# Feed-forward products as seven half-size block products, with x streamed from DRAM

## The chip, the cores and the metric

One Trainium2 chip, one program on all 8 cores (two dies, cores 0 to 3 and 4 to 7). The time is device microseconds of the slowest core. Most executions agree within a few tenths of a per cent; in some, cores of one die run at a lower granted TensorE clock and the time is longer. Those are called slow runs here and are not compared with fast ones.

## The reference

Two layers of a diffusion backbone; in each, four token mixers run side by side and a squared-ReLU MLP follows. Each core takes its own 1280 tokens (1024 context, 256 latent) through all the weights.

```python
D_MODEL = 2048; D_FF = 4 * D_MODEL
def _layer(x, cond, lw, h0, lat):
    mod = (jax.nn.silu(cond) @ w_mod + b_mod)[:, None, :]      # 6 D values: "modulation"
    sh1, sc1, g1, sh2, sc2, g2 = jnp.split(mod, 6, axis=-1)
    h = _rms(x) * (1 + sc1) + sh1
    proj = h @ w_in
    ...   # four mixers, their gates, and the merge
    x = x + g1 * (merged @ w_out)
    h2 = _rms(x) * (1 + sc2) + sh2
    x = x + g2 * (jnp.square(jax.nn.relu(h2 @ w_ff1)) @ w_ff2)  # the feed-forward
    return x, k, v, s_fin
```

## The kernel before

The program writes operations with priorities; a list scheduler of its own orders them on every engine and places semaphores. Activations lie as feature blocks (partitions) by 1280 tokens, in f16; x in f32 (80 KB a partition) stays in SBUF during the feed-forward. A weight block of 128 rows comes through a ring of buffers, cast from f32 by the GpSimd queue.

```python
NRING = 7
def dense(srcs, act, evac, group=1, ...):       # per block: 16 matmuls each of 512, 512, 256 columns
    ...
    for tgi, (t0, n) in enumerate(TGS):
        dense_tile(ws[0], W16, act, t0, n, evac, g[0][0], tgi, ...)
    if hook is not None: hook()                 # hk = mod_step: a modulation round after each block

# feed-forward of a layer: four quarters of D_FF, up (w1) then down (w2)
for q in range(4):
    dense(b1, hT, ev_f1, tag="ff1", hook=hk)                    # 16 blocks: relu^2 into mT
    dense(b2, mT, ev_res(l, 80, None), tag="ff2", hook=hk)      # 16 blocks: x = psum*g2 + x
    ...   # first stage in groups of five blocks; last stage with norm and output

def mod_kc(l, s, kc, st):                       # a modulation round: 1 MB of w_mod, 4 small matmuls
    w = ring(wm[l, s, kc], tag="wmod")
    ...
    if kc == 15:
        tm = A(180 + 8, [16, 32], F32)          # its transpose: a tile shared with other scratch
...
# start: load x, sums of squares, 32 modulation rounds, then normalise
mod_step(32)
for tgi in range(3): norm_tile(0, 0, tgi)
...
S.pools["ps"].allow = {..., "d": (4, 5, 6, 7), "s": (0, 1, 2), "g": (4, 6), "mod": (3,), "G": (4, 6, 0, 2)}
```

Of the kernel before, what the change touches and what calls it, by code (L numbers as in the profile page):

```python
# [40 lines left out]
class Pool:  # L41
    def __init__(self, n, view, psum=False):
        self.n = n
        self.view = view
        self.psum = psum
        self.free = [0.0] * n
        self.busy = [False] * n
        self.last = [None] * n
        self.live = {}
        self.quota = {}  # L50
        self.allow = {}
        self.seq = None
        self.ptr = 0

    def take(self, vt):
        if self.seq is not None and self.seq[self.ptr] is not vt:
            return False
        c = vt.cls
        if c in self.quota and self.live.get(c, 0) + vt.nb > self.quota[c]:
            return False  # L60
        best = None
        for s in self.allow.get(c) or range(0, self.n - vt.nb + 1, vt.nb):
            if any(self.busy[s + i] for i in range(vt.nb)):
                continue
            k = max(self.free[s + i] for i in range(vt.nb))
            if best is None or k < best[0]:
                best = (k, s)
        if best is None:
            return False
        s = best[1]  # L70
        self.ptr += 1
        vt.slot = s
        vt.prev = []
        for i in range(vt.nb):
            self.busy[s + i] = True
            if self.last[s + i] is not None:
                vt.prev.append(self.last[s + i])
            self.last[s + i] = vt
        self.live[c] = self.live.get(c, 0) + vt.nb
        return True  # L80
# [12 lines left out]
class Graph:  # L93
# [123 lines left out]
    def schedule(self):  # L217
        ops = self.ops
        for o in list(ops):
            for v in o.new:  # L220
                if self.pools[v.pool].psum:
                    mine = set(v.ops)
                    for i in v.ops:
                        if ops[i].eng != "pe":
                            o.preds.update(p for p in ops[i].preds if p not in mine and p < o.id)
        for pool in self.pools.values():
            if not pool.psum:
# [249 lines left out]
NRING = 7  # L477
TOTKB = 207.5
# [37 lines left out]
def build():  # L516
# [39 lines left out]
    with es:  # L556
# [52 lines left out]
        acc1 = cal([768], F32)  # L609
# [5 lines left out]
        keep = cal([2, 10])  # L615
        lsm = cal([202])
# [5 lines left out]
        mhalf = cal([16])  # L622
        dtv = cal([10, 16])
        dtA = cal([10, 16])
        E = cal([6, 10, 8])
        wgt = cal([2, 10, 8])
        ssn = cal([2, 10])
        stt = [cal([10]) for _ in range(6)]
        ssv = [cal([2]) for _ in range(8)]
        assert cb[0] <= TOTKB  # L630

        xT = A(40, [16, T], F32)
# [4 lines left out]
        tmpi = [0]  # L637

        def tmp16(dt=F16):
            tmpi[0] = (tmpi[0] + 1) % 4  # L640
            v = TMP[tmpi[0]]
            return v if dt == F16 else v.bitcast(dt)
# [9 lines left out]
        def load(dst, src, nb, q="sp", r=(), w=None, prio=None, tag="ld"):  # L652
            S.dma(q, dst, src, nb, r=r, w=[dst] if w is None else w, prio=(S.p if prio is None else prio) - 60.0, tag=tag)
# [27 lines left out]
        def dense(srcs, act, evac, group=1, tag="mm", hook=None, cls="D"):  # L681

            i = 0
            while i < len(srcs):
# [8 lines left out]
                else:  # L693
# [3 lines left out]
                    for (b, s), w in zip(g, ws):  # L697
                        for tgi in (1, 2):
                            dense_tile(w, W16, act, TGS[tgi][0], TGS[tgi][1], evac, b, tgi, tag=tag, cls=cls)
                        S.p += UNIT * 0.6  # L700
# [84 lines left out]
        def mod_kc(l, s, kc, st):  # L785
# [3 lines left out]
            w = ring(wm[l, s, kc], tag="wmod")  # L789

            def f(e):
                ins = None
                for j in range(4):
                    ins = e.matmul(ps.ap()[32 * j:32 * j + 32, :], lhsT=scT[:, kc, :], rhs=w.ap(F16)[:, 512 * j:512 * j + 512], start=kc == 0, stop=kc == 15)  # L794
                return ins
            S.op("pe", 0.24, f, r=[w, scT], w=[ps], tag="mod")
            if kc == 15:
                tm = A(180 + 8, [16, 32], F32)
# [20 lines left out]


        acc0 = A(38, [512], F32)

        def accv(a, b):
            return acc0[:, a:b] if b <= 512 else acc1[:, a - 512:b - 512]

        def sq_acc(fc, t0, n, first):
            t = tmp16(BF16)[:, 0:n]
            xv = xT[:, fc, t0:t0 + n]
            av = accv(t0, t0 + n)
            if first:  # L830
                act_op(av, xv, AF.Square, n, [xv], [av])
            else:
                act_op(t, xv, AF.Square, n, [xv], [t])
                tt("dve", av, av, t, ALU.add, n, [av, t], [av])

        def norm_rstd(c0, c1, k):

            nck = c1 - c0
            ps = PS("n")

            def f(e):
                ins = None
                for c in range(c0, c1):
                    ins = e.matmul(ps.ap()[:, c - c0:c - c0 + 1], lhsT=accv(c * 128, c * 128 + 128), rhs=ones_f[:, 0:1], start=True, stop=True)  # L844
                return ins
            S.op("pe", 0.3 * nck, f, r=[accv(c0 * 128, c1 * 128), ones_f], w=[ps], tag="norm")
# [3 lines left out]
            S.op("pool", 0.6, lambda e: e.tensor_tensor(out=rv, in0=sv, in1=mhalf[:, 0:nck], op=ALU.pow), r=[sv, mhalf], w=[rv])  # L850
            ps2 = PS("n")
            for c in range(c0, c1):
                dg = tmp16(F32)[:, 0:128]
# [4 lines left out]
        def norm_apply(l, which, t0, n, ps2):  # L858
            jsh, jsc = (0, 16) if which == 0 else (48, 64)
            s = 0 if t0 < 1024 else 1  # L860
            for fc in range(16):
                t = tmp16()[:, 0:n]
# [7 lines left out]
        def norm_tile(l, which, tgi):  # L870
            t0, n = TGS[tgi]
            ps2 = norm_rstd(t0 // 128, (t0 + n) // 128, tgi)
            norm_apply(l, which, t0, n, ps2)
# [154 lines left out]
        def fourier(l):  # L1028
            alt = [0]

# [3 lines left out]
            dense([(g, wf[l, g]) for g in range(4)], hT, ev, tag="fproj", cls="d")  # L1034
# [62 lines left out]
        def gmlp(l):  # L1097
# [4 lines left out]
            def vt(t):  # L1102
# [3 lines left out]
                S.p += 3.5  # L1106
                vg = gelu2(ps, 512, None, "gelv")
# [9 lines left out]
            for b in range(4):  # L1117
                dense([(b, wu[l, b])], hT, ev_u, tag="uproj", cls="d")
# [20 lines left out]
        def ssm_proj(l):  # L1139
# [22 lines left out]
            dense([(b, wx[l, b]) for b in (4, 5, 6, 7, 0, 1, 2, 3)], hT, ev, tag="xproj", cls="d")  # L1162
# [10 lines left out]
            for t in range(NT):  # L1173
# [3 lines left out]
                S.p += 3.5  # L1177
                zv = ztok[:, t, :]
# [297 lines left out]
        def reload_x(fcs, l):  # L1476
            for fc in fcs:
                load(xT[:, fc, :], (xin if l == 0 else xs)[fc], 128 * T * 4, r=[] if l == 0 else ["xs%d" % fc], tag="xld")

        def layer(l):  # L1480
            last = l == NL - 1
            S.tag = "mix"
            layer_consts(l)
            attn_proj(l)
# [9 lines left out]
            hk = mod_step  # L1494
# [4 lines left out]
            reload_x(order, l)  # L1499
# [3 lines left out]
            def after_o(blk, tgi, t0, n):  # L1503
                sq_acc(blk, t0, n, tgi not in seen)
                seen.add(tgi)
                if blk == order[-1] and tgi in (0, 2):
                    if tgi == 0:
                        norm_tile(l, 1, 0)
                    else:
                        norm_tile(l, 1, 1)  # L1510
                        norm_tile(l, 1, 2)
            ev = ev_res(l, 32, after_o)
            dense([(b, wo[l, b]) for b in order[:11]], mT, ev, tag="wout", hook=hk)
            dense([(b, wo[l, b]) for b in order[11:]], mT, ev, group=5, tag="wout", hook=hk)
            while modq and modq[0][0] == l:
                mod_step()
            if not last:
                mod_push(l + 1, range(6))
            seen2 = set()

            def ev_f1(blk, tgi, t0, n, ps):
                r = tmp16()[:, 0:n]
                act_op(r, lambda: ps.ap()[:, 0:n], AF.Relu, n, [ps], [r], boost=BOOST)
                a = mT[:, blk, t0:t0 + n]
                stt_(a, r, 1.0 / 16, r, ALU.mult, ALU.mult, n, [r], [a], boost=BOOST)

            def after_f(blk, tgi, t0, n):
                if last:
                    S.dma("sp", y_o[blk][:, t0:t0 + n], xT[:, blk, t0:t0 + n], 128 * n * 4, r=[xT[:, blk, t0:t0 + n]])
                    return  # L1530
                sq_acc(blk, t0, n, tgi not in seen2)
                seen2.add(tgi)
                S.dma("sp", xs[blk][:, t0:t0 + n], xT[:, blk, t0:t0 + n], 128 * n * 4, r=[xT[:, blk, t0:t0 + n]], w=["xs%d" % blk] if tgi == 0 else ["xs%d" % blk])
                if blk == 15 and tgi in (0, 2):
                    if tgi == 0:
                        norm_tile(l + 1, 0, 0)
                    else:
                        norm_tile(l + 1, 0, 1)
                        norm_tile(l + 1, 0, 2)
            for q in range(4):  # L1540
                b1 = [(b, w1[l, q * 16 + b]) for b in range(16)]
                if q == 0:
                    dense(b1[:5], hT, ev_f1, group=5, tag="ff1", hook=hk)
                    dense(b1[5:], hT, ev_f1, tag="ff1", hook=hk)
                else:
                    dense(b1, hT, ev_f1, tag="ff1", hook=hk)
                b2 = [(b, w2[l, q, b]) for b in range(16)]
                if q < 3:
                    dense(b2, mT, ev_res(l, 80, None), tag="ff2", hook=hk)
                else:  # L1550
                    while modq:
                        mod_step()
                    e2 = ev_res(l, 80, after_f)
                    dense(b2[:11], mT, e2, tag="ff2")
                    dense(b2[11:], mT, e2, group=1 if last else 5, tag="ff2")

        setup()
        for fc in range(16):
# [3 lines left out]
        for fc in range(16):  # L1562
            for tgi, (t0, n) in enumerate(TGS):
                sq_acc(fc, t0, n, fc == 0)
        mod_step(32)
        for tgi in range(3):
            norm_tile(0, 0, tgi)
        mod_push(0, (2, 3, 4, 5))
        for l in range(NL):
            layer(l)  # L1570
        S.pools["ps"].allow = {"as": (0,), "av": (2, 3), "d": (4, 5, 6, 7), "s": (0, 1, 2), "g": (4, 6), "mod": (3,), "G": (4, 6, 0, 2)}
# [222 lines left out]
```

## Time and profile before

| | kernel before |
|---|---|
| time | 5205 us median of three runs |
| TensorE busy | 95% of the span |
| feed-forward, layer 0 / layer 1 | 1178 / 1165 us, counted from the norm in front of it; TensorE without a gap once the hole after that norm is over |
| mixers, layer 0 / layer 1 | 555 / 551 us |
| gates, merge and output projection, layer 0 / layer 1 | 746 / 717 us (at full clock) |
| start to first attention projection | 215 us |

The feed-forward is 45% of the span and, but for these holes, purely TensorE. The lines that carry this are in the prediction. One more, on the start: a table of 20 us windows (columns: window, length, then busy us and instructions of PE, PEld, DVE, ACT, POOL; granted clock, DMA share, GB/s).

```profile
60.00:80.00 20.00, 7.40 (x48) 4.65 (x48) 7.44 (x19) 4.87 (x11) 5.36 (x9) 1.00 0.56 111
80.00:100.00 20.00, 3.73 (x28) 0.90 (x28) 0.00 (x0) 0.00 (x0) 3.17 (x6) 1.00 1.04 166
100.00:120.00 20.00, 4.29 (x28) 0.92 (x28) 0.98 (x3) 0.00 (x0) 3.51 (x7) 1.00 1.03 172
```

DMA is saturated from 80 us on with modulation weights. There is a short dip from 60 to 80 us, where x has come and the norm runs.

### The profile page before, as it was taken

What the parts mean: (1) busy time and instruction counts of PE and PEld (TensorE: products, weight loads), DVE (VectorE), ACT (ScalarE), POOL (GpSimd) and SP (SyncE); (2) the same over time, 40 slices, a digit from 0 to 9 for tenths busy, and PEclk for the clock granted to TensorE, in tenths of its full rate; (3) what the DMA queues carried; (4) which work ended last, traced back from release to release, by engine and by line L of the source; (5) the groups of instructions that cost most, each with busy time, mean ns of one, the idle gap of its engine ahead of it and who ended that gap; (6) DMA issues with size and microseconds to landing.
All of it is one profiled execution on the core that took longest, in us unless ns stands there. A gap on an engine that the chain in (4) does not pass through costs nothing.

```text
span 5229.1 us, 71536 instructions; the slowest of 8 cores (5194.4 to 5229.1 us)
## 1 busy us (share of the span) xinstructions
PE 4942.5 (95%) x27836; PEld 2557.1 (49%) x27836; DVE 1803.3 (34%) x3060; ACT 1128.2 (22%) x2062; POOL 684.1 (13%) x1044
## 2 busy tenths in 40 slices
PE   1699989999998999999998998999999899999999
PEld 0334444455554555555554344455555455555555
DVE  2446681122242222222245467522223422222222
ACT  1356341111122010010123654311111310101010
POOL 1220241111101111111004013300000000000000
PEclk9999998899998999999999999999999899999999
DMA  9431356665645666666353321544334233333334
GB/s 198 96 69 28 59 124 127 122 132 109 117 79 91 115 117 117 114 119 111 65 137 71 59 46 32 126 91 100 61 63 94 47 62 61 61 61 61 61 66 112
DMA packets 168954, 468.01 MB, mean 90 GB/s; under 512 B 18736, under 2 KB 54064, under 8 KB 168368
## 3 DMA queue, kind: packets, MB, share of 16 engines
q0 software_dynamic: 106560, 368.10, 40.3%
q1 hardware_dynamic: 62064, 95.34, 5.6%
q8 instruction: 228, 3.74, 0.3%
q14 instruction: 102, 0.84, 0.1%
HBM read 792.09 MB, written 39.32 MB: 159 GB/s over the span
## 4 chain that ended last, share of the span: by engine, by line
PE 87%; DVE 3%; issue 3%; DMA 3%; POOL 2%; ACT 1%; SPq 1%; DVEq 0%; POOLq 0%; ACTq 0%
PE psum L664 81%; DVE arena L724 2%; DMA arena<-wm 1%; PE psum L1059 1%; PE psum L794 1%; PE psum L999 1%; PE psum L1017 1%; POOL arena L947 1%; ACT arena L714 1%; PE psum L1019 1%; SPq L215 1%; DVE arena L728 1%; DMA arena<-lc 1%; DMA arena<-wf 0%; POOL arena L724 0%
## 5 line engine op out<-in xcount | busy, mean ns | idle before, releaser
L664 PE MATMUL psum<-arena 128*128 128x512 f16 (+1 forms) x24320 | 4533.1, 347 | 37.6 <-ACT arena L714 15.1
L664 PEld LDWEIGHTS psum<-arena 128*128 128x128 f16 x24320 | 2367.1, 98 | 2105.8 <-issue 231.1
L714 ACT ACTIVATE arena<-psum 128x512 f16<-128x512 f32 (+4 forms) x970 | 515.9, 532 | 3132.9 <-PE psum L664 3043.2
L728 DVE SCALAR_TENSOR_TENSOR arena<-arena 128x512 f16<-128x512 f16 (+8 forms) x569 | 369.9, 656 | 957.3 <-ACT arena L714 924.7
L728 DVE SCALAR_TENSOR_TENSOR arena<-arena,psum 128x512 f16<-128x512 f16 (+4 forms) x492 | 297.9, 606 | 1040.7 <-ACT arena L714 1039.9
L728 DVE SCALAR_TENSOR_TENSOR arena<-psum,arena 128x512 f32<-128x512 f32 (+1 forms) x480 | 316.7, 661 | 890.5 <-PE psum L664 889.2
L724 DVE TENSOR_TENSOR arena<-arena 128x512 f32<-128x512 f32 (+7 forms) x796 | 454.4, 589 | 192.2 <-ACT arena L714 126.5
L714 ACT ACTIVATE arena<-arena 128x512 f16<-128x512 f16 (+8 forms) x489 | 297.6, 652 | 515.4 <-DVE arena L728 317.4
L215 POOL DMA_DIRECT2D arena<-w x256 | 136.0, 531 | 1319.7 <-PE psum L664 1269.1
L215 POOL DMA_DIRECT2D arena<-wm x192 | 103.2, 540 | 1173.7 <-PE psum L794 1020.5
L714 ACT ACTIVATE arena<-psum,arena 128x512 bf16<-128x512 f32 x320 | 202.3, 684 | 128.0 <-PE psum L999 127.8
L724 POOL TENSOR_TENSOR arena<-arena 128x512 bf16<-128x512 bf16 (+2 forms) x160 | 183.9, 1167 | 194.8 <-DVE arena L724 97.7
L215 POOL DMA_DIRECT2D arena<-wg x128 | 72.6, 569 | 862.0 <-PE psum L664 570.1
L794 PE MATMUL psum<-arena 128*32 128x512 f16 x768 | 84.0, 434 | 75.0 <-DMA arena<-wm 74.4
L724 DVE TENSOR_TENSOR arena<-arena,psum 128x512 f16<-128x512 f32 (+2 forms) x232 | 130.6, 607 | 24.0 <-PE psum L855 20.4
L738 ACT COPY arena<-psum 128x512 f16<-128x512 f16 (+5 forms) x148 | 70.1, 491 | 117.1 <-PE psum L664 36.7
L724 DVE TENSOR_TENSOR arena<-psum,arena 128x512 f32<-128x512 f32 (+3 forms) x166 | 80.7, 503 | 41.9 <-POOL arena L947 36.0
L794 PEld LDWEIGHTS psum<-arena 128*32 128x32 f16 x768 | 20.9, 95 | 134.8 <-issue 134.7
L739 DVE CAST arena<-psum 128x512 f16<-128x512 f32 (+4 forms) x102 | 52.6, 523 | 93.5 <-PE psum L1059 73.0
L844 PE MATMUL psum<-arena 128*128 128x1 f32 x80 | 12.5, 274 | 71.0 <-DVE arena L724 68.0
L1024 DVE RECIPROCAL arena<-psum 128x256 f32<-128x256 f32 x40 | 70.2, 1755 | 10.5 <-PE psum L1019 9.7
L1017 PE MATMUL psum<-arena 128*64 128x512 bf16 (+1 forms) x352 | 68.2, 387 | 0.0
(87 smaller groups left out, 918.9 us busy)
## 6 DMA issues: line engine op xcount, KB each, us to landing
arena<-w POOLq DMA_DIRECT2D x256, 512.0 KB, 5.3
arena<-wm POOLq DMA_DIRECT2D x192, 512.0 KB, 6.2
arena<-wg POOLq DMA_DIRECT2D x128, 512.0 KB, 6.8
arena<-xin SPq DMA_DIRECT2D x32, 640.0 KB, 20.4
arena<-wb POOLq DMA_DIRECT2D x64, 256.0 KB, 7.2
arena<-wo POOLq DMA_DIRECT2D x32, 512.0 KB, 5.3
arena<-xs SPq DMA_DIRECT2D x16, 640.0 KB, 7.1
arena<-dftA SPq DMA_DIRECT2D x16, 512.0 KB, 11.9
```

The costliest lines, as they stand in the source:

```text
L215: return self.op(q, issue, (lambda e, o=out, a=in_, k=kw: e.dma_start(out=lz(o), in_=lz(a), **k)), r, w, prio, dma=nbytes, q=q, tag=tag)
L664: ins = e.matmul(o, lhsT=lhs(kc), rhs=rhs(kc), start=kc == 0, stop=kc == nk - 1)
L714: return e.activation(out=lz(o), in_=lz(i), func=func, scale=scale, **kw)
L724: lambda e: e.tensor_tensor(out=lz(o), in0=lz(a), in1=lz(b), op=op), r=r, w=w, prio=S.p - boost, tag=tag)
L728: lambda e: e.scalar_tensor_tensor(out=lz(o), in0=lz(a), scalar=sc, in1=lz(b), op0=op0, op1=op1),
L738: return S.op("act", tact(n), lambda e: e.copy(out=lz(o), in_=lz(i)), r=r, w=w, prio=S.p - boost, tag=tag)
L739: return S.op(eng, tpool(n) if eng == "pool" else tdve(n, ps, x), lambda e: e.tensor_copy(out=lz(o), in_=lz(i)), r=r, w=w, prio=S.p - boos ...
L794: ins = e.matmul(ps.ap()[32 * j:32 * j + 32, :], lhsT=scT[:, kc, :], rhs=w.ap(F16)[:, 512 * j:512 * j + 512], start=kc == 0, stop=kc == 15)
L947: S.op("pool", 0.6, lambda e, rs=rs, ss=ss: e.tensor_tensor(out=rs, in0=ss, in1=mhalf[:, 0:10], op=ALU.pow), r=[ss, mhalf], w=[rs], prio=S ...
L999: ins = e.matmul(sc.ap()[:, hf * 512:hf * 512 + n], lhsT=kT[64 * hf:64 * hf + 64, kb * 128:(kb + 1) * 128], rhs=qT[64 * hf:64 * hf + 64, j ...
L1017: ins = e.matmul(pv.ap()[64 * hf:64 * hf + 64, 0:n], lhsT=V[:, kb, 64 * hf:64 * hf + 64], rhs=PT[:, hf, 0:n], start=ki == 0, stop=ki == nk ...
L1024: S.op("dve", 0.0066 * 256 + 0.1, lambda e, sm=sm, b=b: e.reciprocal(out=rec, in_=sm.ap()[:, 256 * b:256 * b + 256]), r=[sm], w=[rec], tag ...
```

## The change

Intent: take columns off TensorE. Two row blocks of weights (halves A11, A12 and A21, A22) times two halves of the tokens and of the contraction need eight block products. The Winograd form of Strassen's algorithm needs seven, with four sums of weights, four of activations and seven sums of results. A unit of two blocks so becomes 112 matmuls of 320 columns.

The sums of activations take the place of x in SBUF. So x goes to DRAM after the output projection, and the down stages load, update and store it in parts of 128 x 320 elements. To make room and keep engines free, modulation rounds leave the feed-forward, the weight ring shrinks from 7 to 6, scratch tiles and PSUM banks are dealt out anew, and the start is reordered.

```diff
-NRING = 7
+NRING = 6
+        TMX = cal([16, 32])
+        HTs = [A(40 + 10 * i, [8, 640]) for i in range(4)]     # sums of activations, in x's place
+        ATs = [A(80 + 10 * i, [8, 640]) for i in range(4)]
+        SL = [A(184 + 2 * i, [1024]) for i in range(4)]        # sums of weights
+        def sunits(units, act, Ts, epi, pre=None, tag="st"):
+            ...   # next unit's two weight blocks and sums a unit ahead
+                prods = (("X", w8(ra, 0), ra, "B11", True), ("Y", k8(s2), s2, 1, True), ("V", k8(s3), s3, 2, True), ("Z", k8(s1), s1, 0, True),
+                         ("X", w8(ra, 1), ra, "B21", False), ("Z", k8(s4), s4, "B22", False), ("V", w8(rb, 1), rb, 3, False))
+            ...   # each for two token parts of 320; VectorE adds the results
+            XSt = [hT[:, i, 640:1280].bitcast(F32) for i in range(8)]      # buffers for x: one unit
+            def pre_f2(ba, bb):
+                ...   load(XSt[s_ * 4 + k], xs[blk][:, c:c + SUBS], ...)
+            def epi_f2(dst):
+                ...   x = XSt[s_ * 4 + k];  res(x, b, ps, *gcol(blk), c);  spill(blk, c, SUBS, x, dst)
             for q in range(4):
-                    dense(b1, hT, ev_f1, tag="ff1", hook=hk)
-                    dense(b2, mT, ev_res(l, 80, None), tag="ff2", hook=hk)
+                    sunits([pair1(i) for i in range(8)], hT, HTs, epi_f1, tag="sf1")
+                    sunits([pair2(i) for i in range(8)], mT, ATs, epi_f2(...), pre=pre_f2, tag="sf2")
...   modulation: out of the feed-forward
-            hk = mod_step
+            hk = mod_hook                                       # does nothing
+        mod_spread(96, 11.0)                                    # before layer 0's mixers
+                mod_spread(64, 15.0)                            # in layer 1's mixers
-                tm = A(180 + 8, [16, 32], F32)
+                tm = TMX
...   norm: the diagonal for the broadcast is in the same tile
-                dg = tmp16(F32)[:, 0:128]
+                dg = TMX.rearrange("p a b -> p (a b)")[:, 128 * (c - c0):128 * (c - c0) + 128]
...   mixers: Fourier projection first, in a group of four
-        S.pools["ps"].allow = {..., "d": (4, 5, 6, 7), "s": (0, 1, 2), "g": (4, 6), "mod": (3,), "G": (4, 6, 0, 2)}
+        S.pools["ps"].allow = {..., "d": (4, 5, 6), "s": (0, 1, 6), "g": (2, 4), "mod": (7,), "G": (0, 2, 4)}
```

## The prediction

> **What bounds the kernel now.** I read first the page's busy shares and its chain of work that ended last, then a table of busy time by stage, then the matmuls of one long stage by shape, and last the DMA queues.
>
> ```profile
> PE 4942.5 (95%) x27836; PEld 2557.1 (49%) x27836; DVE 1803.3 (34%) x3060; ACT 1128.2 (22%) x2062; POOL 684.1 (13%) x1044
> PE 87%; DVE 3%; issue 3%; DMA 3%; POOL 2%; ACT 1%; SPq 1%; DVEq 0%; POOLq 0%; ACTq 0%
> PE psum L664 81%; DVE arena L724 2%; DMA arena<-wm 1%; PE psum L1059 1%; PE psum L794 1%; PE psum L999 1%; PE psum L1017 1%; POOL arena L947 1%; ACT arena L714 1%; PE psum L1019 1%; SPq L215 1%; DVE arena L728 1%; DMA arena<-lc 1%; DMA arena<-wf 0%; POOL arena L724 0%
> ```
>
> TensorE carries 87% of the chain, the dense matmuls of one helper (L664) 81% of the span. By stage (columns: window, length, busy us and instructions of PE, PEld, DVE, ACT, POOL, granted clock, DMA share, GB/s):
>
> ```profile
> 0.00:160.00 160.00, 24.26 (x152) 9.80 (x152) 33.36 (x85) 26.58 (x53) 22.59 (x44) 1.00 0.96 196
> 195.00:780.00 585.00, 539.79 (x3178) 250.98 (x3177) 364.41 (x558) 266.98 (x489) 169.34 (x199) 0.96 0.34 69
> 780.00:1040.00 260.00, 260.00 (x1330) 128.02 (x1328) 49.76 (x98) 32.74 (x62) 26.91 (x51) 0.89 0.64 127
> 1560.00:1600.00 40.00, 21.32 (x112) 11.31 (x111) 24.73 (x55) 22.98 (x39) 6.07 (x10) 0.66 0.66 114
> 1600.00:2750.00 1150.00, 1149.69 (x6534) 606.07 (x6533) 285.81 (x478) 137.99 (x255) 116.53 (x219) 1.00 0.59 110
> 4068.00:4117.00 49.00, 26.91 (x161) 17.63 (x160) 37.23 (x75) 34.80 (x57) 4.43 (x7) 0.76 0.33 54
> 4117.00:5229.00 1112.00, 1109.36 (x6143) 601.32 (x6141) 242.87 (x384) 101.55 (x194) 63.94 (x121) 1.00 0.37 67
> ```
>
> The feed-forward stages (1600 to 2750, 4117 to 5229) have no idle TensorE time, full clock, VectorE at 22 to 25% and DMA at 37 to 59%. What takes columns away from TensorE there shortens the kernel one for one, until something else fills. Idle TensorE lies elsewhere: in the DMA-bound start (24 busy of 160 us), in the mixers, and in two holes of some 20 us (1560, 4068) between output projection and feed-forward.
>
> The chain in order of time gives the last stage as one piece, 6144 matmuls (128 weight blocks of 32 of 512 columns and 16 of 256) in 1109.97 us: 8.67 us a block, 180.7 ns a matmul.
>
> **What the Trainium skill says.** "TensorE: Matmul & The Clock Gate", section "Wait — 56ns, not 53.3ns?": warm matmuls start every N / 2.4 GHz + 2.5 ns. So 215.8 ns at 512 and 109.2 at 256; two to one that is 180.3, and the trace has 180.7. For 320 columns I take 135.8 ns, an estimate from that section. Part 1 of the page warns that dense matmuls on three cores of a die bring the clock to 13/16 for as long as they last. Here it came in part, 0.89 from 780 to 1040, and in no feed-forward stage with all eight cores dense; I budget full clock there. "VectorE: DVE Perf Modes", section "Mode 2×_1P": 16-bit operands in SBUF give two results a cycle, PSUM and fp32 one. The trace agrees: 441 ns for an f16 sum of 512, 753 in f32. "HBM Reference", section "Specifications": some 358 GB/s for each core when both of a pair stream. From 70 to 150 us the trace had 164 GB/s written as f16, so 328 read, at full DMA share.
>
> **The change part by part.**
>
> 1. Columns. One unit (two row blocks, both token halves) was 2 x 16 x 1280 = 40960 columns in 96 matmuls: 17.31 us. It becomes 7 products x 2 parts x 8 matmuls of 320: 112 x 135.8 ns = 15.21 us. Saved: 2.10 us. Layer 0 has 29 units up and 28 down (6 and 8 blocks stay dense), layer 1 29 and 32: 118 units, **-247 us**, all on the path.
>
> 2. What the products cost elsewhere, in 15.2 us. Durations at 320, 640 and 1024 elements are interpolated from the groups by shape: PSUM multiply-add 750 and 482 ns at 512 and 256, so 549; PSUM sum 681 and 416, so 482; f16 sum 441 and 300, so 511 at 640 and 722 at 1024. VectorE: 10 PSUM sums 4.8 us, 4 weight sums 2.9, and either 4 activation sums 2.0 (up: 9.7 us, 64%) or 8 residuals 4.4 plus 0.4 for the cut at token 1024 (down: 12.5 us, 82%). ScalarE, up: 16 operations of about 0.46 and 2 copies, 8.3 us. All below 15.2, beside TensorE.
>
> 3. x from DRAM. A down unit loads and stores 8 parts of 164 KB: 2.62 MB, beside two weights of 0.52 MB (as written). The queues of before:
>
> ```profile
> q0 software_dynamic: 106560, 368.10, 40.3%
> q1 hardware_dynamic: 62064, 95.34, 5.6%
> ```
>
> The casting queue moved 368.1 MB in 40.3% of 5229 us, 175 GB/s when busy; the plain one 326 GB/s. A down unit so takes 6.0 + 8.0 = 14.0 us of DMA in 15.2 (92%), an up unit 40%. HBM: 2.1 + 2.6 MB in 15.2 us, 310 GB/s a core, under the 358. It fits, barely. A reload needs its buffer's store to land (2 to 3 us here), yet is used a whole unit later; weights are fetched a unit ahead; up stages work off a backlog.
>
> 4. PSUM. A unit holds all 8 banks, but the banks which a product takes were last read at least two products (4.3 us) before, and a bank read in between and added to again has one product of slack. Evacuations are 0.5 to 1.1 us. I allow **+10 us** at the eight passages from up to down, where the last activation sums are needed about 2 us after their inputs, and **+20 us** for DMA and VectorE bursts in 56 streamed units, some 0.35 us each.
>
> 5. The two holes. At 1567 TensorE waits until 1592: the first up matmuls stand behind norm work, because both use the same four scratch tiles. The change gives them their own tiles and norms each token group by itself; five blocks of the first group (80 x 215.9 ns = 17.3 us) now lie over the rest. I take 20 of some 25 us each: **-40 us**.
>
> 6. The start. It stays DMA-bound: 0.96 share to 160 us, same bytes, so the modulation ends near 145 instead of 153. x is scaled by the norm during the wait, and the rest goes to two engines. The attention projections began at 211; I put them at about 185: **-25 us**.
>
> 7. Modulation of later steps: 160 rounds of 4 small matmuls. Each costs 0.42 us among dense work (9.09 us from block to block in layer 0, 8.67 in layer 1). The order of instructions has 96 of them inside layer 0's feed-forward before and none after; about 60 go into the mixers, whose gaps hide a part: **-15 us**.
>
> 8. The mixers lose one of four PSUM banks for projections (given to modulation) and the gate merge one of four bank pairs; the ring of weights shrinks from 7 to 6. **+10 us**.
>
> Sum: 5205 - 247 + 30 - 40 - 25 - 15 + 10 = 4918; I say **4915 us**, 5.6% less.
>
> **The rivals.**
>
> - The down stages become bound by DMA or VectorE. For: 92% and 82% worked out; VectorE is in order, so a late x holds the PSUM sums behind it. Against: a unit of prefetch, and up stages at 40%. If 56 units took 17 us, as dense, the time would be about 5010.
> - The clock: busier neighbours bring the 13/16 state into the product stages. For: it appears here from 780 to 1040. Against: the gate merge from 1040 had random dense data at 0.58 DMA share and clock 1.00. At 0.89 over 1795 us of products it costs 220 us: about 5130.
> - The chain of additions behind each product stalls TensorE by half a microsecond a unit: +60 us, about 4975. Against: the slack of part 4.
> - The other way: holes and modulation vanish wholly, no stall: about 4865.
>
> **Range and chances.** The columns are arithmetic; the side gains have an uncertainty of some 30 us, stalls another 40, mostly upward. So 4855 to 4990. Faster than 5101 fails only under the clock rival or two rivals at once: faster 0.96, within 2% 0.03, slower 0.01.
>
> **What would show it.** Right: 13216 matmuls of 320 columns at 135 to 137 ns each, units of 15.2 to 15.6 us with TensorE fully busy; DMA near 0.9 in down stages, 0.4 in up stages, VectorE near 80 and 65%; no wait over 5 us at either hole; attention projections by 190 us. Wrong: TensorE waits on VectorE or on x inside down stages, their units above 16 us; clock under 0.97 in product stages; mixers longer than 585 and 630 us.

## The result and the profile after

The changed kernel took 5009 us (median of four runs, the slow one of 5124 us among them; fast runs 4995.94, 5005.90, 5012.84). Before, in the same rounds: fast runs 5204.38, 5205.36 and 5234.69 us. The ratio is 0.960, 95% interval 0.956 to 0.965. A ratio here is the mean time of one kernel's fast runs over that of the other's of the same rounds, so not quite the ratio of the medians. A second job gave 0.962 (0.956 to 0.968). So the kernel is 4% faster, where the prediction had 5.6%, and 5009 us, like every single run, lies above its range of 4855 to 4990 us.

The page of the changed kernel:

```profile
PE 4663.9 (93%) x29724; PEld 2736.0 (55%) x29724; DVE 2584.2 (52%) x4975; ACT 1465.2 (29%) x2951; POOL 696.3 (14%) x1044
...
q0 software_dynamic: 106560, 368.10, 44.4%
q1 hardware_dynamic: 200304, 263.18, 16.9%
...
PE 74%; DMA 12%; DVE 5%; issue 4%; POOL 2%; SPq 1%; ACT 1%; another core or an unknown queue 0%; DVEq 0%; POOLq 0%; ACTq 0%
PE psum L684 42%; PE psum L1623 25%; DMA xs<-arena 6%; DVE arena L744 3%; DMA arena<-xs 3%; DMA arena<-wm 2%; PE psum L1114 1%; SPq L222 1%; DVE arena L748 1%; PE psum L1053 1%; DMA arena<-xin 1%; PE psum L820 1%; PE psum L1071 1%; ACT arena L734 1%; POOL arena L1001 1%
...
L1623 PE MATMUL psum<-arena 128*128 128x320 f16 x13216 | 1807.3, 299 | 35.8 <-DVE arena L744 25.3
...
arena<-xs SPq DMA_DIRECT2D x448, 160.0 KB, 5.4
...
xs<-arena SPq DMA_DIRECT2D x384, 160.0 KB, 6.5
```

L1623 are the new products, L684 the dense helper. The 13216 matmuls are there (118 units of 112). TensorE fell from 87 to 74% of the chain, and DMA rose from 3 to 12%: stores of x (6%) and loads of x (3%) are on the path, which were not there at all. The last two lines give the median time from issue to landing: 5.4 us for the loads and 6.5 us for the stores.

Windows of the changed kernel (columns as before; core 1, the slowest), in order: mixers of layer 0, the two places where the holes were, and two down stages.

```profile
226.00:796.00 570.00, 517.68 (x3124) 237.48 (x3122) 356.28 (x545) 261.60 (x476) 182.36 (x219) 0.97 0.45 85
...
1560.00:1600.00 40.00, 40.00 (x225) 22.55 (x224) 27.05 (x59) 30.35 (x55) 4.54 (x7) 1.00 0.46 99
...
3968.00:4010.00 42.00, 42.00 (x235) 23.54 (x234) 28.71 (x64) 31.98 (x59) 4.50 (x7) 1.00 0.47 98
...
4110.00:4225.00 115.00, 114.16 (x840) 81.75 (x839) 79.63 (x171) 12.97 (x30) 8.06 (x15) 1.00 0.85 198
...
4355.00:4465.00 110.00, 104.90 (x768) 74.32 (x767) 69.66 (x149) 12.13 (x28) 7.53 (x14) 1.00 0.78 181
```

The holes are gone (40 busy of 40 us, 42 of 42). The down stages have full clock, DMA at 0.78 to 0.85 and VectorE at 63 to 69%, both below what the prediction had, and still TensorE loses time there.

Where the time went, by stage. The mean over the cores of the duration between two landmarks among the matmuls: the first of 272 columns (attention projections), the last of 128 columns before the gates, the first of the norm's sums of squares (for the gates of layer 0 before, die 1 alone, since die 0 ran at a clock of about 0.9 there), in us:

| stage | before | after | difference | predicted |
|---|---|---|---|---|
| start to attention projections | 214.8 | 224.4 | +10 | -25 |
| mixers, layer 0 | 555.3 | 569.7 | +14 | |
| gates to output projection, layer 0 | 745.8 | 751.0 | +5 | |
| feed-forward, layer 0 | 1178.0 | 1025.1 | -153 | |
| norm to attention, layer 1 | 72.5 | 77.2 | +5 | |
| mixers, layer 1 | 551.5 | 571.0 | +20 | |
| gates to output projection, layer 1 | 717.5 | 733.6 | +16 | |
| feed-forward, layer 1 | 1165.2 | 1031.5 | -134 | |
| both feed-forwards | | | -287 | -297 (247 columns, 40 holes, 40 modulation, less 30 stalls) |
| mixers, gates and the norm between | | | +60 | +35 (25 modulation, 10 banks and ring) |
| sum | | | -217 | -287 |

The feed-forward did nearly what was predicted. 70 us went elsewhere: 35 in the start, 25 in mixers and gates, 10 in the feed-forward. The rest of the distance is the choice of the slowest core: the fast runs before had it 5 us above this table's mean of 5201, the profiled run after 11 us above 4984, since the cores now stall at different times.

The start. Windows of the changed kernel, and then its TensorE instructions in order of time (start, length, instruction, in brackets what it waited for):

```profile
80.00:100.00 20.00, 3.81 (x17) 3.79 (x18) 6.64 (x20) 5.27 (x13) 1.04 (x1) 1.00 0.53 144
100.00:120.00 20.00, 13.26 (x84) 7.55 (x83) 14.28 (x31) 0.00 (x0) 5.65 (x10) 1.00 0.09 14
...
160.00:180.00 20.00, 3.08 (x20) 0.69 (x20) 2.99 (x8) 2.02 (x3) 3.10 (x6) 0.50 1.04 184
```

```profile
94.58 1.83 PE L896 MATMUL psum<-arena 128*128 128x1 f32 x8 [94.58 <-DVE arena L744]
...
99.72 0.78 PE L907 MATMUL psum<-arena 128*128 128x128 f32 x2
...
114.01 0.76 PE L907 MATMUL psum<-arena 128*128 128x128 f32 x2 [0.54 <-DVE arena L753]
114.70 1.90 PE L820 MATMUL psum<-arena 128*32 128x512 f16 x16
```

From 100 to 120 us DMA is at 0.09: idle, in the one stage that is bound by DMA. The first modulation matmuls (L820) start only at 114.7 us, behind all matmuls of the norm (L896 and L907), which themselves wait for x until 94.6 us. All 15 buffers for modulation weights are full by then, and none comes free before L820 has read it.

The down stages. First the waits of SyncE's queue, which issues loads and stores of x, then those of VectorE, both from 4110 to 4225 us (engine, line, waited for: us in total, times, longest):

```profile
SPq L436 <- DVE arena L748: 84.2, 5, 81.5
SPq L438 <- DMA xs<-arena: 38.4, 21, 4.6
```

```profile
DVE arena L748 <- DMA arena<-xs: 18.2, 12, 3.8
DVE arena L744 <- PE psum L1623: 12.1, 15, 2.2
```

The queue waits 38 us of 115 for stores to land before it may load into the same buffer (the 81.5 us of the first line began before this window, in the up stage). VectorE in turn waits 18 us for x. An example from VectorE's instructions in order of time, 4396 to 4401 us:

```profile
4396.11 0.48 DVE L744 TENSOR_TENSOR arena<-psum,arena 128x320 f32<-128x320 f32 x1
4400.47 0.55 DVE L748 SCALAR_TENSOR_TENSOR arena<-arena 128x320 f32<-128x320 f32 x1 [3.88 <-DMA arena<-xs]
```

For 3.88 us a late x holds up VectorE, and with it the sums behind it for which TensorE needs its banks. In the whole program TensorE waits 25 us for those sums (the page's line of L1623).

### The profile page after: what moved, and what is told of

Its sections match the earlier page's. It is cut to its first block, busy times and chain, and to the rows that moved or that the text cites. A ratio compares the mean times of both kernels' runs of the same rounds, so it can differ in the third digit from the quotient of the medians.

```text
span 4994.4 us, 84152 instructions; the slowest of 8 cores (4969.1 to 4994.4 us)
## 1 busy us (share of the span) xinstructions
PE 4663.9 (93%) x29724; PEld 2736.0 (55%) x29724; DVE 2584.2 (52%) x4975; ACT 1465.2 (29%) x2951; POOL 696.3 (14%) x1044
## 3 DMA queue, kind: packets, MB, share of 16 engines
q0 software_dynamic: 106560, 368.10, 44.4%
q1 hardware_dynamic: 200304, 263.18, 16.9%
## 4 chain that ended last, share of the span: by engine, by line
PE 74%; DMA 12%; DVE 5%; issue 4%; POOL 2%; SPq 1%; ACT 1%; another core or an unknown queue 0%; DVEq 0%; POOLq 0%; ACTq 0%
PE psum L684 42%; PE psum L1623 25%; DMA xs<-arena 6%; DVE arena L744 3%; DMA arena<-xs 3%; DMA arena<-wm 2%; PE psum L1114 1%; SPq L222 1%; DVE arena L748 1%; PE psum L1053 1%; DMA arena<-xin 1%; PE psum L820 1%; PE psum L1071 1%; ACT arena L734 1%; POOL arena L1001 1%
## 5 line engine op out<-in xcount | busy, mean ns | idle before, releaser
L684 PE MATMUL psum<-arena 128*128 128x512 f16 (+2 forms) x12992 | 2452.2, 347 | 23.9 <-ACT arena L734 10.7
L684 PEld LDWEIGHTS psum<-arena 128*128 128x128 f16 x12992 | 1252.4, 98 | 1115.3 <-issue 109.9
L1623 PE MATMUL psum<-arena 128*128 128x320 f16 x13216 | 1807.3, 299 | 35.8 <-DVE arena L744 25.3
L1623 PEld LDWEIGHTS psum<-arena 128*128 128x128 f16 x13216 | 1290.6, 98 | 552.0 <-issue 51.5
L744 DVE TENSOR_TENSOR arena<-arena 128x1024 f16<-128x1024 f16 (+9 forms) x1648 | 923.6, 579 | 237.1 <-ACT arena L734 144.3
L734 ACT ACTIVATE arena<-arena 128x320 f32<-128x320 f32 (+8 forms) x1374 | 680.9, 518 | 893.6 <-DVE arena L744 458.8
L744 DVE TENSOR_TENSOR arena<-psum,arena 128x320 f32<-128x320 f32 (+4 forms) x1346 | 656.6, 490 | 426.8 <-PE psum L1623 304.7
L748 DVE SCALAR_TENSOR_TENSOR arena<-arena,psum 128x512 f16<-128x512 f16 (+3 forms) x492 | 298.3, 607 | 1044.4 <-ACT arena L734 1044.0
L734 ACT ACTIVATE arena<-psum 128x512 f16<-128x512 f32 (+6 forms) x738 | 382.9, 520 | 1390.0 <-PE psum L684 1305.4
L758 ACT COPY arena<-psum 128x320 f32<-128x320 f32 (+6 forms) x384 | 170.0, 448 | 1026.8 <-DVE arena L748 547.1
L748 DVE SCALAR_TENSOR_TENSOR arena<-arena 128x320 f32<-128x320 f32 (+10 forms) x665 | 354.7, 554 | 217.8 <-DMA arena<-xs 131.3
L820 PE MATMUL psum<-arena 128*32 128x512 f16 x768 | 80.0, 424 | 62.5 <-DMA arena<-wm 49.4
L896 PE MATMUL psum<-arena 128*128 128x1 f32 x80 | 11.9, 267 | 96.2 <-DVE arena L744 94.6
L820 PEld LDWEIGHTS psum<-arena 128*32 128x32 f16 x768 | 21.1, 97 | 129.6 <-issue 128.4
```

The costliest lines, as they stand in the source:

```text
L684: ins = e.matmul(o, lhsT=lhs(kc), rhs=rhs(kc), start=kc == 0, stop=kc == nk - 1)
L734: return e.activation(out=lz(o), in_=lz(i), func=func, scale=scale, **kw)
L744: lambda e: e.tensor_tensor(out=lz(o), in0=lz(a), in1=lz(b), op=op), r=r, w=w, prio=S.p - boost, tag=tag)
L748: lambda e: e.scalar_tensor_tensor(out=lz(o), in0=lz(a), scalar=sc, in1=lz(b), op0=op0, op1=op1),
L758: return S.op("act", tact(n), lambda e: e.copy(out=lz(o), in_=lz(i)), r=r, w=w, prio=S.p - boost, tag=tag)
L820: ins = e.matmul(ps.ap()[32 * j:32 * j + 32, :], lhsT=scT[:, kc, :], rhs=w[:, 512 * j:512 * j + 512], start=kc == 0, stop=kc == 15)
```

## The experiments

"Stall" means here: the sum over all products of a core of the time between two starts beyond 135.8 ns (some 2 us of it come from the trace's whole nanoseconds). In the changed kernel it was 36 to 51 us a core in the repeat, 43 in the mean.

**The changed kernel again.**

> The changed kernel again, beside the experiments on the same chip. Expected about 5005 us, ratio to the kernel before 0.960, attention projections from 225 us, up units of products 15.21 us each, down units 15.2 to 16.6.

Ratio 0.962; cores 4970 to 5003 us, lowest run 5004 us; attention projections at 218 to 223 us. It is what the next runs are set beside.

**The start: an own tile for the modulation transposes.**

```diff
-                tm = TMX
+                tm = A(28, [16, 32], F32) if l == 0 and s < 2 else TMX
```

> Only the transposes of the first two modulation steps get a scratch tile of their own. Theory: in the changed kernel the 32 first modulation matmuls stand behind ten norm matmuls because both use one scratch tile, so their 15 buffers do not come free and the DMA engines idle from 88 to 118 us. Then the DMA idle goes, the attention projections begin at about 195 instead of 225 us, and the time falls by 25 to 32 us. Rival: the start is bound by the bytes, and x merely lands later because more modulation loads share the engines with it; then the projections still begin after 218 us and the time falls by less than 8 us.

All timed runs were slow, so there is no ratio. In the profiled run die 1 had full clock (0.984 to 0.986): spans 4940 to 4971 us against 4981 to 5003 on die 1 in the repeat (4970 to 4999 on its die 0), and attention projections at 193 to 195 us instead of 218 to 223. Its windows (core 5):

```profile
80.00:100.00 20.00, 3.56 (x28) 2.25 (x24) 5.36 (x17) 4.16 (x11) 1.58 (x3) 1.00 1.02 215
100.00:120.00 20.00, 13.01 (x77) 7.53 (x70) 8.86 (x23) 0.00 (x0) 8.55 (x14) 0.66 1.04 174
```

DMA stays at 1.02 and 1.04 where it had been 0.53 and 0.09. So the shared scratch tile was the cause: the transpose of a modulation step writes the tile that holds the norm's diagonals, the scheduler put the modulation matmuls behind the norm, and DMA ran dry. About 27 us.

**No stream of x** (wrong: x is loaded once a layer and stored only at the end).

```diff
+                if ba or once.get(0):
+                    return
...
-                    spill(blk, c, SUBS, x, dst)
+                    if dst is not None:
+                        spill(blk, c, SUBS, x, dst)
```

> Wrong result on purpose: x is loaded once a layer into the down stages and neither reloaded nor stored for the next units, VectorE and TensorE work unchanged. Theory (the stalls of the down stages are late x, through the store, reload chain of one in-order queue): down units fall to 15.2 to 15.3 us, stalls of products from about 40 to under 15 us, the spread between cores from some 25 to under 12 us, the time falls by 35 to 55 us. Rival (VectorE at 82% is the cause): stalls stay above 30 us and the time falls by less than 10 us.

Cores 4941 to 4961 us (lowest run 4962). All units, up and down, but those of layer 0's last stage took 15.21 us, the stall fell to 10 us, the feed-forwards to 1011-1013 and 1015 us. So the stream costs some 33 us of stall; the products themselves, with all their sums on VectorE, cost none beyond a unit's 15.21 us.

**Dense feed-forward, the rest of the change kept.**

```diff
-                    sunits([pair1(i) for i in range(8)], hT, HTs, epi_f1, tag="sf1")
-                    sunits([pair2(i) for i in range(8)], mT, ATs, epi_f2(None if q < 3 else y_o), pre=pre_f2, tag="sf2")
+                dense(b1[k:], hT, ev_f1, tag="ff1")
+                    dense(b2, mT, ev_res(l, 80, None), tag="ff2")
```

> The changed kernel with its feed-forward products undone: dense blocks with x resident, everything else of the change kept (start, own scratch tiles, banks, modulation in the mixers). Theory: seven products are worth 247 us of columns less some 45 us of stalls, so this run takes 195 to 210 us more than the changed kernel, 5195 to 5215 us, and all the other parts together are worth within 25 us of nothing against the kernel before. Rival (the products gained less than their columns, and the other parts the rest): it takes less than 5170 us.

Lowest run 5185 us, cores 5171 to 5184, between the two expectations. Feed-forwards 1114 and 1140 us: without the products the change gains 64 us in layer 0 (40 modulation, 24 hole) and 25 in layer 1 (hole). The products gain the remaining 89 and 108 us: 197, which is 247 less the stall of 43, within 7 us.

**Stores of x on ScalarE's queue.**

```diff
-            S.dma("sp", d[fc][:, t0:t0 + n], src, ...)
+            S.dma(q, d[fc][:, t0:t0 + n], src, ...)
-                    spill(blk, c, SUBS, x, dst)
+                    spill(blk, c, SUBS, x, dst, "act")
```

> The stores of x in the down stages are issued by ScalarE's queue instead of SyncE's, so a load of x no longer stands behind a store that waits for VectorE. Everything else as in the changed kernel (5009 us, TensorE stalled 34 to 51 us a core inside the products). Theory (the in-order queue holds the loads back): stalls fall below 25 us, the units of the last down stage of layer 0 come from 16.7-17.1 under 16.2, the time falls by 10 to 30 us. Rival (the transfers themselves are short of bandwidth, or the store's landing alone sets it): stalls stay at 35 us or more and the time within 8 us of the changed kernel.

Slow profile; on die 1 at full clock the stalls were 11 to 35 us, 27 in the mean, against 43. The last down stage of layer 0 stayed at 16.7-17.1 us a unit. The only fast run took 4977 us. Neither theory as written: the in-order queue was some 17 us of it, not all.

**Both of these together.**

> e7_actq plus the own tile for the modulation transposes of the first two steps (e1_start, which began the attention projections at 193-195 us instead of 219-223). If the two causes are separate, their gains add: attention projections at 195 us, product stalls as in e7_actq, time some 28 us below e7_actq, so 4945 to 4975 us. Rival (the slowest core or a later wait swallows the earlier start): under 12 us below e7_actq.

Fast runs 4960, 4960 and 4977 us (too few fast runs of the kernel before for a ratio), cores of the profiled one 4925 to 4959; attention projections at 193 to 196 us, stall 15 to 32 us, 26 in the mean. The lowest runs lie 17 us apart (4960 and 4977), the cores at full clock 29 in the mean (4941 and 4970, profiled runs). By the cores the two causes add, as expected; the slowest core shows less of it.

**Twice the buffers for x** (8 more, in a quarter of mT that the down products don't read).

```diff
-            XSt = [hT[:, i, 640:1280].bitcast(F32) for i in range(8)]
+            XSt = [hT[:, i, 640:1280].bitcast(F32) for i in range(8)] + [mT[:, i, 640:1280].bitcast(F32) for i in range(8)]
-                        load(XSt[s_ * 4 + k], xs[blk][:, c:c + SUBS], ...)
+                        load(XSt[8 * (ba % 2) + s_ * 4 + k], xs[blk][:, c:c + SUBS], ...)
-                    x = XSt[s_ * 4 + k]
+                    x = XSt[8 * (blk % 2) + s_ * 4 + k]
```

> Twice as many buffers for x in the down stages (16 instead of 8, the free quarter of the activations added); same bytes, same queue, same order of work on TensorE, VectorE, ScalarE and GpSimd. In the changed kernel a load of x needs the landing of the store from the same buffer one unit before (6.5 + 5.4 us of a 15.2 us unit, plus the queue); now two units before. Theory (the chain of store and load is too long for one unit, not the bandwidth): stalls of the products fall from 34-51 us to below 20 us a core, of which 7 us are in the last down stage of layer 0; time 20 to 35 us below the changed kernel. Rival (the DMA queues are short of bandwidth in the down stages, share 0.78 to 0.85): stalls stay above 30 us, time within 8 us.

Ratio 0.960 (0.953 to 0.967), lowest run 4975 us. Die 1 was throttled in part in the profiled run, which hides the gain in the ratio; die 0 at full clock spans 4943 to 4972 us against 4970 to 4999 for its cores in the repeat. Stalls there: 12 to 25 us, 19 in the mean, of which some 7 in layer 0's last stage; all down units of the streamed stages took 15.2 us on that die, but for one last unit of 15.8, and the rest of the stall moved to the first two up units after a down stage (up to 23 us a unit), which was not examined. VectorE's waits in a down stage of layer 1 (core 3):

```profile
DVE arena L744 <- PE psum L1623: 21.9, 27, 1.9
DVE arena L748 <- DVE arena L744: 4.0, 23, 0.2
DVE arena L748 <- DMA xs<-arena: 0.3, 2, 0.2
```

The wait for x is gone, with the same bytes through the same queue. So bandwidth was not short; the chain of store and load within one unit was too long.

**Twice the buffers and the start's own tile.**

> e9_deep plus the own tile for the modulation transposes of the first two steps. If the two causes are separate and there is no third of their size: attention projections at 195 us, stalls as in e9_deep, 4930 to 4955 us on the slowest core, the best version so far. Rival (something else then sets the end, such as the spread between cores): 4960 us or more.

Ratio 0.951 (0.947 to 0.955), fast runs 4956 and 4940 us, cores 4921 to 4955, stall 10 to 22 us, attention projections at 194 to 196 us. Correct, and the best version of all: some 55 us below the changed kernel. The higher of the two runs lost time on cores 6 and 7 in the mixers (584 and 586 us, clock 0.98 over the span).

**VectorE relieved of the sums of weights** (wrong).

```diff
-            tt("dve", s1, q(rb, 0), q(rb, 1), ALU.add, 1024, [rb], [s1], x=2)
-            ...   # and the three others
+            for v in SL:
+                mset(v, 0.01, 1024)          # once a layer
```

> Wrong on purpose: the four sums of weights of each unit are not computed (constant tiles in their place), which takes about 2.9 us of VectorE out of each 15.2 us unit. Theory (the stalls inside the down stages come from the stream of x): stalls of the products stay above 30 us a core and the time within 10 us of the changed kernel. Rival (VectorE is too full in the down stages, 82% worked out): stalls fall below 15 us and the time by 20 us or more.

Lowest run 5009 us; stalls 41 to 65 us, no less than with the sums. VectorE's load is not the cause. With one exception: the last stage of layer 0, where VectorE also sums squares for the next norm, went from 17.1 to 15.38 us a unit. There, in 4 of 118 units, VectorE's load counts, for 7 us.

**Modulation rounds out of the mixers.**

```diff
-        mod_spread(96, 11.0)                  # before layer 0's mixers
-                mod_spread(64, 15.0)          # in layer 1's
+                mod_spread(96, 6.5)           # both after the mixers, before the gates
+                mod_spread(64, 9.0)
```

> The modulation rounds are moved out of the mixers to after them (gates, merge, output projection). Mixers took 570 and 570-575 us in the changed kernel, 555 and 552 in the one before. Theory (rounds of 0.42 us inside the mixers, 35 and 25 of them, are not hidden there): mixers return to some 556 and 560 us and the stages after them grow by as much, the time within 10 us. Rival (one PSUM bank fewer for the projections): mixers stay at 567 us or more, and the stages after them grow all the same, so the time rises by 10 to 25 us.

A miss for both: mixers 561 to 566 and 557 to 561 us at full clock, so 6 and 11 us shorter in the mean, but gates 772 to 788 and 749 to 757 us, 15 to 37 us longer. Fast runs 5030 to 5065 us, slower than the changed kernel. Crowding the rounds costs more than they cost in the mixers.

**That, with the fourth PSUM bank for projections.**

```diff
-  "d": (4, 5, 6),
+  "d": (4, 5, 6, 7),
```

> e2_mods (modulation rounds after the mixers) plus the fourth PSUM bank for the projections of the mixers, as in the kernel before. e2_mods had mixers of 561-566 and 557-561 us, against 570 and 570-575 in the changed kernel and 555 and 552 before. Theory (the rest of the lengthening is the missing bank): mixers 553 to 558 and 550 to 555 us. Rival (the rest has another cause, such as the scratch tiles that moved): mixers as in e2_mods, 560 us or more.

Mixers at full clock 564 to 573 and 562 to 563 us: no gain. But the rounds still shared that bank, so this doesn't clear the banks.

**No later modulation rounds** (wrong: constants in place of 160 of the 192 rounds).

```diff
+            if l == 1 or s >= 2:
+                if kc == 15:
+                    ...   mset(modT[l][:, c, 16 * s:16 * s + 16], 0.01, 16)
+                return
```

> Wrong on purpose: of the 192 modulation rounds the 160 after the start are left out (their results are constants), with their 1 MB loads. The kernel before had 8 of them in the mixers and 56 in the gates of layer 0, and 0 and 0 in layer 1; the changed one 34 and 60, and 23 and 40. Theory (the rounds make the mixers and gates longer): mixers fall from 570 and 571 to 548-556 us in both layers, gates of layer 1 from 733 to some 717, gates of layer 0 from 750 to some 725; the time falls by 65 to 85 us. Rival (in the mixers it is the ring of six weight buffers or the missing PSUM bank): mixers stay at 562 us or more in both layers, and the time falls by less than 50 us.

Slow profile; on cores at full clock in the stage: mixers 560 us in layer 0, gates 716-718 and 718-720 us. For the mixers of layer 1 the best cores had 564-567 us at clock 0.93 to 0.94, against 0.96 to 0.97 else, so this is read high (a fast run below, otherwise alike, has 562-564). So the rounds cost 10 and 6 to 7 us in the mixers, 34 and 15 in the gates. In the mixers the theory held for half at best; 5 us remain in layer 0 and about 12 in layer 1 against before. Fast runs 4950 and 4980 us: some 40 us less than the changed kernel, where the stages sum to 65. Most of the difference is the slowest core: the mean of the cores was 4922 us in the run of 4950, 61 below the changed kernel's 4984.

**That, with all PSUM banks as before.**

> e12_norounds (wrong on purpose, no modulation rounds after the start) with the whole allotment of PSUM banks of the kernel before. Theory (banks): the mixers fall from 560 and 565 us to 551-556 us in both layers, on cores at full clock. Rival (ring of weights, or the order of instructions): 559 us or more.

At full clock: mixers 557 to 562 us in layer 0, no change, and 557 to 559 in layer 1, some 5 to 7 us less (against the run below and e12). The banks are about half of what remained in layer 1.

**That (e12), with five weight buffers in the ring.**

```diff
-NRING = 6
+NRING = 5
```

> e12_norounds with five weight buffers in the ring in place of six. Theory (the ring is what lengthened the mixers when it went from 7 to 6): mixers grow by another 5 to 15 us, to 566 us or more in layer 0 and 570 or more in layer 1, on cores at full clock. Rival (banks): mixers stay within 3 us of 560 and 565.

All cores at full clock: mixers 560-561 and 562-564 us, no longer than with six. The ring is not it, as far as one step down shows: seven to six was not tried, nor a run with the rounds in. Some 5 us in layer 0 and 7 in layer 1 stay open; the mixers' order was changed too (the Fourier projection now comes first, in a group of four blocks), which was not tried by itself.

## Why the prediction was right and wrong

The steps that failed: part 6, which took the start to be bound by the bytes alone (35 us off); then parts 7 and 8, what the mixers and gates pay for moved rounds and fewer banks (with an unforeseen 5 us before layer 1, 25 us off); and the stall of the stream in parts 3 and 4 (about 10 us off). The saving of columns, the core of the change, came as predicted.

- **Part 1, columns (-247): right.** Up units took 15.21 us, exactly 112 x 135.8 ns (all but the first after a down stage, up to 20 us on some cores), the figure taken from the Trainium skill's "TensorE: Matmul & The Clock Gate". The run with a dense feed-forward gives the products 197 us net, as the columns less the measured stall would have it.
- **Part 2, work beside TensorE: right in size.** PSUM sums took 487 to 490 ns (482 worked out), sums of weights 682 (722), residuals 552 (549). With no stream of x all this lay beside the products without stall, but for the last four down units of layer 0.
- **Parts 3 and 4, the stream (+30): mechanism named, size off by 13 us.** It said that a reload needs its store to land, put that at 2 to 3 us, and looked for the limit in bandwidth. The bandwidth did suffice (share 0.78 to 0.85 instead of 0.92). But the store took 6.5 us and the load 5.4: 11.9 of the 15.2 us from one use of a buffer to the next, the wait in the queue not counted. So its sign of being wrong came: TensorE stalled inside down stages, single units well above 16 us. The 10 us allowed for the passages from up to down were not needed: the last up unit of a stage took 15.21 us, and without the stream the passages show no stall. Twice the buffers took off 24 us of 43, another queue for the stores 17; both at once was not tried. Why a load takes so long is open in part. The Trainium skill's "DMA: Bandwidth & Descriptors", section "Queues, rings and completion order", says that an engine takes turns between queues and drains a whole packet, typically 9 to 17 descriptors, before it switches. In the trace, from 4396.0 to 4398.5 us on core 1, with both queues at work, 91 packets of weights (4096 bytes) and 88 of x (1280 bytes, one row) started, as many of the one as of the other. How long a single turn is it does not show, since it names no engine. The page's shares give 67 ns for a packet of the plain queue (0.169 x 16 x 4994 us / 200304) and 333 ns for one of the casting queue (0.444 x 16 x 4994 us / 106560). A part of x is 128 rows, 8 for each of 16 engines: with as many packets of weights between them that is some 3.2 us, an estimate, of the 5.4 and 6.5. No run isolates it.
- **Part 5, holes (-40): right.** They shrank from about 29 and 30 us of lost TensorE time to about 7 each, 45 in all.
- **Part 6, the start (-25): the step that failed most.** It measured +10, 35 us off. It said "It stays DMA-bound: 0.96 share to 160 us", from the same bytes. It did not ask when the buffers of those bytes come free. TMX serves both the norm and the modulation, modulation matmuls went behind the norm, and DMA idled from 91 to 118 us. With an own tile the projections began at 194 us, still 9 us after the 185 of the prediction. The order of instructions on TensorE, which could be read before the run, would have told it: norm matmuls stand first.
- **Part 7, modulation (-15): about -9.** 40 us saved in the feed-forward, as said. By the run without rounds, the 96 that moved cost some 31 us in their new places (8 and 6 in the mixers, 15 in layer 1's gates, 2 in layer 0's, worked out as the share of moved rounds in each stage's cost), where the prediction had 25.
- **Part 8, banks and ring (+10): about +20, a third explained.** 5 to 7 us are the banks, in layer 1; a ring smaller by one more buffer added nothing; the rest is open. The 5 us more between the norm and the attention of layer 1 were not predicted and not examined.
- **The rivals.** DMA or VectorE as bound of the down stages: refuted in 56 of the 60 down units, true of VectorE in four. The chain of additions: no stall without the stream, in all units but those four. The clock: not in the changed kernel's fast runs (0.98 over the span, 0.99 to 1.00 in the feed-forwards of the profiled one). Slow runs had it, on one die at a time mostly, before and after alike.

## What to carry to other kernels

When a stage is bound by transfers, ask for each buffer who frees it and what stands before that reader in its engine's order; equal bytes don't mean equal time. When data go out and come back through the same buffer, add up landing, queue and landing against the time from one use to the next, with the landing times that a busy DMA shows; here a second set of buffers was worth 24 us where the bandwidth had sufficed. And work moved "into gaps" has to be charged for what it costs in the place it goes to, which only a run without it shows.

## What the Trainium skill lacked or had wrong

- "DMA: Bandwidth & Descriptors" gives about 2 us of fixed cost for a transfer that GpSimd issues ("Anatomy of one DMA"). What a small transfer of SyncE's queue takes beside a busy casting queue is not there, and it is more: here 5.4 us for a load and 6.5 us for a store of 160 KB in rows of 1280 bytes, while stores of 256 KB in quieter stages took 3.9 us.
- "TensorE: Matmul & The Clock Gate", Part 1, has the 13/16 clock come once three cores of a die run dense matmuls and hold while the load lasts. In fast runs all eight cores ran dense feed-forwards of over 1000 us at clock 0.99 to 1.00. In slow runs units took 18.38 instead of 15.21 us for whole stages, often on one die while the other stayed at 15.21. The page has it take the whole die; here it came by pairs of cores: in the slow profile of the run with stores on ScalarE's queue, cores 0 and 1 had clock 0.81 through layer 1's feed-forward (1223 us) and cores 2 and 3 clock 1.00 (1022 and 1015 us). So the load alone does not decide it, as that page's wording suggests; what does, no run here shows.
